# One-hot factors of a gate table in pair-major order, and products of two token pairs in one operation

## The chip, the cores and the metric

The kernel runs on one core of a Trainium2 chip. The metric is the device time of one execution in microseconds (us); the median of several runs is compared. The engines of a core work from queues of their own and meet at semaphores: PE (TensorE) multiplies matrices, with its weight loads shown as PEld; DVE (VectorE), ACT (ScalarE) and POOL (GpSimd) work element by element; SP issues most DMAs.

## The reference, cut to what matters

One decoder layer on 528 positions (16 learned ones and 512 tokens) of width 1024: a mixer (a chunked state-space scan beside a gated short convolution), then a retrieval feed-forward, then a norm. The change lies in the feed-forward, `peer_ffn`:

```python
s = einsum('thsd,hskd->thsk', q, sub_keys)          # 8 heads, 2 halves, 128 keys
v_half, i_half = top_k(s, 16)
cand = v_half[:, :, 0, :, None] + v_half[:, :, 1, None, :]
best, pos = top_k(cand.reshape(T, 8, 256), 16)
i1 = take_along_axis(i_half[:, :, 0], pos // 16);  i2 = take_along_axis(i_half[:, :, 1], pos % 16)
experts = i1 * 128 + i2                             # 8 x 16 = 128 of 16384 experts per token
gates = softmax(best)
act = gelu(einsum('td,tkd->tk', x, expert_u[experts])) * gates
out = einsum('tk,tkd->td', act, expert_v[experts])
```

## The kernel before, in words

The mixer takes the first 450 us or so. The feed-forward treats the tokens in four tiles of 128. Tile 0 is done sparsely: its experts' rows are fetched by indirect DMA (`fetch`, `dot`, `weigh`, `addv`). Tiles 1 to 3, 384 tokens, are done densely: for each of 128 blocks b of 128 experts, `z_unit` computes gelu(u_b x) for all 384 tokens (24 matmuls at L699, one activation at L775), multiplies it by the gates of that block (`h_unit`), and multiplies by v_b (`vmm`, L1009). Where an expert isn't among a token's 128, its gate is zero.

So the dense part needs a table of gates, experts by tokens, in DRAM (`gd`). It is made tile by tile, in two steps:

- `select(tt)` finds the lists of a tile (the first index i1, the second i2, the gate, for 128 slots a token), transposes them so that slots lie on partitions, and builds one-hot factors in f16. i1 is cut into its high part xa (0 to 7) and low part xb (0 to 15). `ob` is the one-hot of xb (16 x 128 tokens), `oa` that of xa (8 x 128), and `oag` is oa times the gate, once with the gate's high f16 part and once with its low part (16 x 128). `x2` holds i2.
- `gates(tt, c)` takes 16 tokens at a time (a chunk, TC = 16; 8 chunks a tile, 24 in all), in four groups of four. For every two groups one DVE operation makes `o2`, the one-hot of i2 over 128 keys (L886). For every group DVE makes `o1`, per slot the products oag x ob of four tokens, 512 numbers a pair of tokens. Then for each token two matmuls (L898, one for each part of the gate) contract over the slots, and give that token's 128 x 128 gates in PSUM; ACT copies them into `stg` (L901), and SP writes a chunk's stg into `gd` (L902).

Tokens are handled in pairs that lie next to each other in memory, 4 bytes in f16. `o1` has NO1 = 4 buffers of four tokens, the PSUM tile `pR` six, `stg` two. The factor tiles are stored with tokens innermost, [slot, x, token]; the step tables they are compared with are `iota16` (16 x 128) and `iota128` (128 x 2), both made by POOL.

While the tables are made, dense blocks go on as far as there is room: 36 blocks (`EARLYZ`) are computed early. Five come before the first chunk, 26 are spread over the 24 chunks, and five follow the last chunk (`z_early`, in the driver loop). Their weights are split into a high and a low part as they arrive (`Stream.prep_upto`: ACT at L88, then DVE or POOL at L90). The rest of `select` for the next tile is interleaved with the first chunks of a tile (L836 to L841 are its lookups by one-hot).

Within an engine, instructions run in the order in which the program was scheduled; the scheduler places them by its own estimate of when each can run. So a change in one operation can move its neighbours. PE's queue interleaves L898 with L699, DVE's the products with the splits and the selection.

Of the kernel before, what the change touches and what calls it, by code (L numbers as in the profile page):

```python
# [8 lines left out]
F16 = mybir.dt.float16  # L9
# [3 lines left out]
ALU = mybir.AluOpType  # L13
# [4 lines left out]
P = 128  # L18
# [653 lines left out]
def peer(tc, top, nc, st, small, dram, h, n2s, rs2, g_ffn_row, ident, keys, uv, g_final, out, rstd_of):  # L672
    dma = nc.sync.dma_start
    act = nc.scalar.activation
    V = nc.vector
# [12 lines left out]
    rp = r1.enter_context(tc.tile_pool(name="rp", bufs=2))  # L688
    psR = r1.enter_context(tc.tile_pool(name="psR", bufs=6, space=PSUM, reuse_waits="tile"))

    def proj(kind, b, spans):
        ps = [psZ.tile([P, T], F32, name="pZ") for _ in spans]
        cnt = [0] * len(spans)
        for i in range(2):
            wp = st.next((kind, b), i)
            for s, (o0, o1) in enumerate(spans):
                for k in range(4):
                    for a_, b_ in PASSES:
                        mm(ps[s][:, :o1 - o0], wp[a_][:, k * P:(k + 1) * P], n2s[b_][:, 4 * i + k, o0:o1],  # L699
                           start=cnt[s] == 0, stop=cnt[s] == 23)  # L700
                        cnt[s] += 1
        return ps

    iota128 = rp.tile([P, P, 2], F16, name="iota128", bufs=1)
    nc.gpsimd.iota(iota128, pattern=[[1, P], [0, 2]], base=0, channel_multiplier=0,
                   allow_small_or_imprecise_dtypes=True)
    iota16 = rp.tile([P, 16, P], F16, name="iota16", bufs=1)
    nc.gpsimd.iota(iota16, pattern=[[1, 16], [0, P]], base=0, channel_multiplier=0,
                   allow_small_or_imprecise_dtypes=True)
# [14 lines left out]
    def top2(tt, j):  # L724
        best, pos, cand = bests[tt][:, j], poss[tt][:, j], cands.pop((tt, j))
        V.max(best[:, 0:8], cand)
        V.max_index(pos[:, 0:8], best[:, 0:8], cand)
        V.match_replace(cand, best[:, 0:8], cand, -3.0e38)
        V.max(best[:, 8:16], cand)
        V.max_index(pos[:, 8:16], best[:, 8:16], cand)  # L730
# [13 lines left out]
    for j in range(16):  # L744
        kt = qp.tile([P, P], F32, name="kt")
        dma(out=kt, in_=keys[j])
        p = qps.pop(j) if j in qps else proj("q", j, ((0, T),))[0]
        qT = qp.tile([P, T], F32, name="qT")
        act(qT, p, AF.Copy)
        p = psR.tile([P, 512], F32, name="pR")  # L750
# [16 lines left out]
    rp = r1.enter_context(tc.tile_pool(name="rp3", bufs=2))  # L767
# [23 lines left out]
    def ut_(nm, n=P):  # L791
        return rp.tile([P, n], U32, name=nm, bufs=1)

    def ft(nm, n=P):
        return rp.tile([P, n], F32, name=nm, bufs=1)
# [4 lines left out]
    def select(tt):  # L800
        x16, best, pos = x16s[tt], bests[tt], poss[tt]
        xT = rp.tile([P, 2, 16, 8], F16, name="xT", bufs=1)
        nc.gpsimd.tensor_copy(xT, x16.rearrange("p (h s) x -> p s x h", s=2))
        if tt in EARLY:
            top2(tt, 7)
        else:
            for j in range(8):
                cand2(tt, j, V)
                top2(tt, j)
                if j % 3 == 2:  # L810
                    yield
        lists = rp.tile([P, 3, P], F32, name="lists", bufs=1)

        def kh(ap):
            return ap.rearrange("p (k h) -> p h k", h=8)

        def hk(ap):
            return ap.rearrange("p (h k) -> p h k", k=16)

        pf = pos.rearrange("p h k -> p (h k)")  # L820
        pe, pa, pd, pb = ut_("pe"), ut_("pa"), ut_("pd"), ut_("pb")
        V.tensor_scalar(pe, pf, 2, None, ALU.logical_shift_right)
        V.tensor_scalar(pa, pf, 4, None, ALU.logical_shift_right)
        V.tensor_scalar(pd, pf, 12, None, ALU.bitwise_and)
        V.tensor_scalar(pb, pf, 15, None, ALU.bitwise_and)
        m, t_, u_ = ft("pm"), ft("pt"), ft("pu")
        ij = rp.tile([P, 2, P], F16, name="ij", bufs=1)
        V.tensor_scalar(m, pf, 64.0, None, ALU.is_ge)
        V.scalar_tensor_tensor(t_, pe, -12.0, pa, ALU.add, ALU.subtract)
        V.tensor_tensor(t_, t_, m, ALU.mult)  # L830
        V.tensor_tensor(kh(ij[:, 0]), hk(t_), hk(pa), ALU.add)
        V.tensor_tensor(u_, pd, m, ALU.mult)
        V.tensor_tensor(kh(ij[:, 1]), hk(pb), hk(u_), ALU.subtract)
        for s in range(2):
            oh = rp.tile([P, 16, P], F16, name="oh", bufs=1)
            V.tensor_tensor(oh, iota16, ij[:, s, None, :].broadcast_to([P, 16, P]), ALU.is_equal)  # L836
            ohv = oh.rearrange("p x (k h) -> p x k h", h=8)
            V.tensor_tensor(ohv, ohv, xT[:, s, :, None, :].broadcast_to([P, 16, 16, 8]), ALU.mult)
            for n in (8, 4, 2):
                V.tensor_tensor(oh[:, 0:n], oh[:, 0:n], oh[:, n:2 * n], ALU.add)  # L840
            V.tensor_tensor(lists[:, s], oh[:, 0], oh[:, 1], ALU.add)  # L841
            yield
        ge = rp.tile([P, 8, 16], F32, name="ge", bufs=1)
        V.tensor_tensor(ge, best, best[:, :, 0:1].broadcast_to([P, 8, 16]), ALU.subtract)
        act(ge, ge, AF.Exp)
        gs = small.tile([P, 8], F32, name="gs")
        V.tensor_reduce(gs, ge, AX.X, ALU.add)
        V.reciprocal(gs, gs)
        V.tensor_tensor(kh(lists[:, 2]), ge, gs[:, :, None].broadcast_to([P, 8, 16]), ALU.mult)
        if tt < NGT:  # L850
            xid = xids[tt]
            V.scalar_tensor_tensor(xid[0], lists[:, 0], float(P), lists[:, 1], ALU.mult, ALU.add)
            nc.gpsimd.tensor_copy(xid[1], lists[:, 2])
            return
        p = psR.tile([P, 512], F32, name="pR")
        for i in range(3):
            nc.tensor.transpose(p[:, i * P:(i + 1) * P], lists[:, i], ident)
        gh, gl = (rp.tile([P, P], F16, name="gh") for _ in range(2))
        act(gh, p[:, 2 * P:3 * P], AF.Copy, scale=GS)
        V.scalar_tensor_tensor(gl, p[:, 2 * P:3 * P], GS, gh, ALU.mult, ALU.subtract)  # L860
        x2 = rp.tile([P, P], F16, name="x2")
        xa, xb = (rp.tile([P, P], F16, name="xa") for _ in range(2))
        act(x2, p[:, P:2 * P], AF.Copy)
        iu, ia = ut_("iu"), ut_("ia")
        V.tensor_copy(iu, p[:, 0:P])
        V.tensor_scalar(ia, iu, 4, None, ALU.logical_shift_right)
        V.tensor_scalar(iu, iu, 15, None, ALU.bitwise_and)
        V.tensor_copy(xa, ia)
        V.tensor_copy(xb, iu)
        ob = rp.tile([P, 16, P], F16, name="ob")  # L870
        V.tensor_tensor(ob, iota16, xb[:, None, :].broadcast_to([P, 16, P]), ALU.is_equal)
        oa = rp.tile([P, 16, P], F16, name="oh", bufs=1)[:, 0:8]
        V.tensor_tensor(oa, iota16[:, 0:8], xa[:, None, :].broadcast_to([P, 8, P]), ALU.is_equal)
        oag = rp.tile([P, 16, P], F16, name="oag")
        for w, g_ in enumerate((gh, gl)):
            V.tensor_tensor(oag[:, 8 * w:8 * w + 8], oa, g_[:, None, :].broadcast_to([P, 8, P]), ALU.mult)
        lts[tt] = (x2, ob, oag)

    def gates(tt, c):
        x2, ob, oag = lts[tt]  # L880
        stg = rp.tile([P, NB, TC], F32, name="stg")
        for q in range(TC // 4):
            t0 = c * TC + 4 * q
            if q % 2 == 0:
                o2 = rp.tile([P, 4, P, 2], F16, name="o2", bufs=2)
                V.tensor_tensor(o2, iota128[:, None].broadcast_to([P, 4, P, 2]),  # L886
                                x2[:, t0:t0 + 8].rearrange("p (q t) -> p q t", t=2)[:, :, None, :]
                                .broadcast_to([P, 4, P, 2]), ALU.is_equal)
            o1 = rp.tile([P, 2, 16, 16, 2], F16, name="o1", bufs=NO1)
            for j in range(2):  # L890
                t1 = t0 + 2 * j
                V.tensor_tensor(o1[:, j], oag[:, :, None, t1:t1 + 2].broadcast_to([P, 16, 16, 2]),  # L892
                                ob[:, None, :, t1:t1 + 2].broadcast_to([P, 16, 16, 2]), ALU.mult)
            p = psR.tile([P, 512], F32, name="pR")
            for i in range(4):
                j = 2 * (q % 2) + i // 2
                for w in range(2):
                    mm(p[:, i * P:(i + 1) * P], o2[:, j, :, i % 2],  # L898
                       o1[:, i // 2, 8 * w:8 * w + 8].rearrange("p a b t -> p (a b) t")[:, :, i % 2],
                       start=w == 0, stop=w == 1)  # L900
            act(stg[:, :, 4 * q:4 * q + 4], p.rearrange("p (t i) -> p i t", t=4), AF.Copy, scale=1.0 / GS)  # L901
        dma(out=gd[(tt - NGT) * (P // TC) + c], in_=stg)  # L902
# [192 lines left out]
```

## Time and profile before

| | |
|---|---|
| median of 3 runs | 1767.74 us (1766.79 to 1767.86) |
| the profiled execution's own time | 1769.16 us |
| its span | 1767.5 us |
| PE busy, DVE busy over the span | 1699.3 us, 1373.0 us |
| product operations L892 | 192, busy 109.7 us |
| gate matmuls L898 | 768, busy 74.1 us |

The span is the time between the first and the last recorded instruction; the execution's time has some overhead around it. Busy time is the time in which an engine had at least one instruction running; instructions of one engine overlap at their ends, so that a mean duration times a count can be more than the busy time. PE's matmuls are pipelined, and a matmul that waits for its weights counts as busy.

### The profile page before, as it was taken

How to read it: one execution, taken by the hardware profiler on the slowest of the kernel's cores; microseconds unless marked ns; L12 is line 12 of the kernel's file. 1: busy time of each engine (PE TensorE's matmuls, PEld its weight loads, DVE VectorE, ACT ScalarE, POOL GpSimd, SP SyncE). 2: the span in 40 equal slices, each digit the busy share in tenths (PEclk: the TensorE clock that was granted, in tenths of full speed). 3: DMA queues.
4: the chain of work that ended last, by engine and by line, in shares of the span. 5: the costliest groups of instructions: out<-in, count | busy, mean ns of one | idle time of the engine just before them, and what ended most of it. 6: DMA issues, size and time to landing. Idle time of an engine off the chain costs nothing.

```text
span 1767.5 us, 27063 instructions
## 1 busy us (share of the span) xinstructions
PE 1699.3 (96%) x9549; PEld 1516.8 (86%) x9549; DVE 1373.0 (78%) x2914; ACT 783.0 (44%) x1546; POOL 602.1 (34%) x540
## 2 busy tenths in 40 slices
PE   7899999999999789889999999999999999999997
PEld 6899998977888777778999999999999999999886
DVE  6756468897599999997787777777878776776876
ACT  7444443355533444545444444443434444444343
POOL 3333235440345310224343333333233333333442
PEclk9999999999999899999999999999999999999999
DMA  4222221135422245557989888888888888898772
GB/s 149 72 72 63 81 84 61 60 120 190 159 96 83 82 146 204 199 196 271 335 319 328 310 299 322 311 292 328 307 306 318 315 319 297 315 324 319 266 250 96
DMA packets 132306, 382.92 MB, mean 217 GB/s; under 512 B 10425, under 2 KB 65337, under 8 KB 112713
## 3 DMA queue, kind: packets, MB, share of 16 engines
q1 hardware_dynamic: 113736, 246.96, 41.1%
q0 software_dynamic: 18432, 134.23, 19.7%
q8 instruction: 75, 1.23, 0.3%
q14 instruction: 63, 0.51, 0.1%
HBM read 351.13 MB, written 30.02 MB: 216 GB/s over the span
## 4 chain that ended last, share of the span: by engine, by line
PE 75%; DVE 20%; issue 2%; ACT 1%; DMA 1%; SPq 0%; POOL 0%; DVEq 0%; ACTq 0%; POOLq 0%
PE pV L1009 30%; PE pZ L699 24%; PE pA L293 8%; DVE o L892 5%; PE pA L433 4%; PE pA L590 4%; DVE w L90 1%; DVE o L886 1%; DVE x L761 1%; DVE w L390 1%; DVE x L758 1%; DVE ssb L759 1%; PE pS L522 1%; DVE v L760 1%; DVE v L757 1%
## 5 line engine op out<-in xcount | busy, mean ns | idle before, releaser
L699 PE MATMUL pZ<-n,w 128*128 128x384 f32 (+1 forms) x3408 | 670.8, 349 | 7.0 <-ACT zg L775 5.8
L699 PEld LDWEIGHTS pZ<-n,w 128*128 128x128 f32 x3408 | 610.2, 190 | 29.4 <-ACT zg L775 6.2
L90 POOL TENSOR_TENSOR w<-raw,w 128x512 fp32r<-128x512 f32 x210 | 301.5, 1440 | 752.0 <-ACT w L88 270.6
L1009 PE MATMUL pV<-w,hh 128*128 128x512 f32 x2304 | 540.7, 390 | 0.0
L90 DVE TENSOR_TENSOR w<-raw,w 128x512 fp32r<-128x512 f32 (+2 forms) x447 | 314.3, 706 | 277.8 <-PE pV L1009 173.5
L88 ACT ACTIVATE w<-raw 128x512 fp32r<-128x512 f32 (+1 forms) x657 | 404.0, 620 | 253.9 <-issue 93.6
L1009 PEld LDWEIGHTS pV<-w,hh 128*128 128x128 f32 x2304 | 431.6, 188 | 86.2
L293 PE MATMUL pA<-nT,w 128*128 128x272 f32 (+3 forms) x1488 | 207.4, 296 | 1.0 <-POOL w L90 0.5
L293 PEld LDWEIGHTS pA<-nT,w 128*128 128x128 f32 (+1 forms) x1488 | 192.1, 188 | 5.9 <-ACT nT L281 0.9
L948 DVE SCALAR_TENSOR_TENSOR h<-row,a,h 128x1024 f32<-128x1024 f32 x128 | 168.8, 1319 | 0.0
L938 DVE SCALAR_TENSOR_TENSOR row<-row,n2k 128x1024 f32<-128x1024 f32 x128 | 159.0, 1245 | 2.1 <-DMA row<-in_uv,xid 2.1
L932 POOL DMA_INDIRECT row<-in_uv,xid x128 | 133.1, 1039 | 24.7 <-issue 7.8
L984 ACT ACTIVATE hh<-hh 128x384 fp32r<-128x384 f32 x128 | 67.3, 525 | 144.8 <-PE pV L1009 89.5
L775 ACT ACTIVATE zg<-pZ 128x384 f32<-128x384 f32 x128 | 62.5, 488 | 139.6 <-PE pZ L699 134.7
L892 DVE TENSOR_TENSOR o<-oag,ob 128x512 f16<-128x512 f16 x192 | 109.7, 628 | 0.0
L898 PE MATMUL pR<-o,o 128*128 128x128 f16 x768 | 74.1, 222 | 20.5 <-DVE o L892 11.4
L898 PEld LDWEIGHTS <-o 128*128 128x128 f16 x768 | 49.2, 98 | 50.6 <-DVE o L892 29.9
L496 POOL TENSOR_TENSOR sr<-aS,ut 128x384 fp32r<-128x384 f32 x64 | 62.8, 999 | 84.7 <-PE pS L498 43.3
L982 DVE TENSOR_TENSOR hh<-zg,gt 128x384 f32<-128x384 f32 x128 | 86.6, 676 | 4.5 <-DMA gt<-gd 1.2
L985 DVE TENSOR_TENSOR hh<-hh 128x384 fp32r<-128x384 f32 x128 | 87.1, 680 | 2.6 <-ACT hh L984 2.4
L943 ACT ACTIVATE a<-z 128x1 f32<-128x1 f32 x128 | 25.9, 202 | 139.9 <-DVE row L938 139.9
L901 ACT ACTIVATE stg<-pR 128x512 f32<-128x512 f32 x96 | 57.0, 598 | 68.7 <-PE pR L898 60.7
(232 smaller groups left out, 1521.1 us busy)
## 6 DMA issues: line engine op xcount, KB each, us to landing
raw<-in_u_t SPq DMA_DIRECT2D x128, 512.0 KB, 4.7
raw<-in_uv SPq DMA_DIRECT2D x128, 512.0 KB, 5.2
gd<-stg SPq DMA_DIRECT2D x24, 1024.0 KB, 6.1
gt<-gd SPq DMA_DIRECT2D x16, 1536.0 KB, 13.3
raw<-in_w_out SPq DMA_DIRECT2D x32, 512.0 KB, 3.5
raw<-in_w_xbc SPq DMA_DIRECT2D x20, 512.0 KB, 3.5
raw<-in_w_q SPq DMA_DIRECT2D x16, 512.0 KB, 3.4
raw<-in_w_z SPq DMA_DIRECT2D x16, 384.0 KB, 3.0
```

The lines of the kernel that those rows point to most:

```text
L88: nc.scalar.activation(hi, r, AF.Copy)
L90: ins = (nc.gpsimd if on_pool else nc.vector).tensor_tensor(lo, r, hi.bitcast(F32), ALU.subtract)
L293: mm(p[:m, :o1 - o0], wp[a][:, c0:c0 + m], nTs[b][:, k, o0:o1], start=i == 0, stop=i == 3 * KD - 1)
L699: mm(ps[s][:, :o1 - o0], wp[a_][:, k * P:(k + 1) * P], n2s[b_][:, 4 * i + k, o0:o1], start=cnt[s] == 0, stop=cnt[s] == 23)
L892: V.tensor_tensor(o1[:, j], oag[:, :, None, t1:t1 + 2].broadcast_to([P, 16, 16, 2]), ob[:, None, :, t1:t1 + 2].broadcast_to([P, 16, 16, 2] ...
L898: mm(p[:, i * P:(i + 1) * P], o2[:, j, :, i % 2], o1[:, i // 2, 8 * w:8 * w + 8].rearrange("p a b t -> p (a b) t")[:, :, i % 2], start=w = ...
L932: nc.gpsimd.indirect_dma_start(out=row.rearrange("p a d -> p (a d)"), out_offset=None, in_=uv, in_offset=bass.IndirectOffsetOnAxis(ap=xids ...
L938: V.scalar_tensor_tensor(row[:, 0], row[:, 0], 1.0, n2k[:, tt], ALU.mult, ALU.mult, accum_out=z)
L948: V.scalar_tensor_tensor(h[:, tt, :], row[:, 1], a, h[:, tt, :], ALU.mult, ALU.add)
L982: V.tensor_tensor(hf_.rearrange("p (c t) -> p c t", t=TC), zg[b].rearrange("p (c t) -> p c t", t=TC), gts[b // GR][:, :, b % GR, :], ALU.mult)
L985: V.tensor_tensor(hl, hf_, hh.bitcast(F32), ALU.subtract)
L1009: mm(acc[tt, nh], hp_[a][:, ts_], vp_[w], start=b == 0 and q == 0, stop=b == NB - 1 and q == 2)
```

## The change

`ob` and `oag` are stored pair-major, [slot, pair of tokens, x, 2], and `oa` in the same way inside the tile of `oh`. They are compared with a small new table `iota2` (16 x 2), broadcast over the 64 pairs, where before `iota16` was used (which `select` still needs for its lookups). The two products of a group, one for each pair, become one operation over both pairs. The shape and layout of `o1`, the matmuls and everything behind them stay as they are.

```diff
+    iota2 = rp.tile([P, 16, 2], F16, name="iota2", bufs=1)
+    nc.gpsimd.iota(iota2, pattern=[[1, 16], [0, 2]], base=0, channel_multiplier=0,
+                   allow_small_or_imprecise_dtypes=True)
...
-        ob = rp.tile([P, 16, P], F16, name="ob")
-        V.tensor_tensor(ob, iota16, xb[:, None, :].broadcast_to([P, 16, P]), ALU.is_equal)
-        oa = rp.tile([P, 16, P], F16, name="oh", bufs=1)[:, 0:8]
-        V.tensor_tensor(oa, iota16[:, 0:8], xa[:, None, :].broadcast_to([P, 8, P]), ALU.is_equal)
-        oag = rp.tile([P, 16, P], F16, name="oag")
+        def pairs(ap, n):
+            return ap.rearrange("p (q t) -> p q t", t=2)[:, :, None, :].broadcast_to([P, P // 2, n, 2])
+
+        def steps(n):
+            return iota2[:, None, 0:n, :].broadcast_to([P, P // 2, n, 2])
+
+        ob = rp.tile([P, P // 2, 16, 2], F16, name="ob")
+        V.tensor_tensor(ob, steps(16), pairs(xb, 16), ALU.is_equal)
+        oa = rp.tile([P, 16, P], F16, name="oh", bufs=1)[:, 0:8].rearrange("p x (q t) -> p (x q t)", t=2)
+        oa = oa.rearrange("p (q x t) -> p q x t", x=8, t=2)
+        V.tensor_tensor(oa, steps(8), pairs(xa, 8), ALU.is_equal)
+        oag = rp.tile([P, P // 2, 16, 2], F16, name="oag")
         for w, g_ in enumerate((gh, gl)):
-            V.tensor_tensor(oag[:, 8 * w:8 * w + 8], oa, g_[:, None, :].broadcast_to([P, 8, P]), ALU.mult)
+            V.tensor_tensor(oag[:, :, 8 * w:8 * w + 8, :], oa, pairs(g_, 8), ALU.mult)
...
-            for j in range(2):
-                t1 = t0 + 2 * j
-                V.tensor_tensor(o1[:, j], oag[:, :, None, t1:t1 + 2].broadcast_to([P, 16, 16, 2]),
-                                ob[:, None, :, t1:t1 + 2].broadcast_to([P, 16, 16, 2]), ALU.mult)
+            V.tensor_tensor(o1, oag[:, t0 // 2:t0 // 2 + 2, :, None, :].broadcast_to([P, 2, 16, 16, 2]),
+                            ob[:, t0 // 2:t0 // 2 + 2, None, :, :].broadcast_to([P, 2, 16, 16, 2]), ALU.mult)
```

Before the changed lines the program's order is the same on every engine, and so it is in the main loop but for its first blocks. In between it moves. DVE's queue in the first tile's second chunk, beside the selection of the next tile, stood so before (tiles by name, a number where several buffers share it; L840 and L841 belong to the selection):

```order
L840 TENSOR_TENSOR oh<-oh 128x1024
L886 TENSOR_TENSOR o_6880<-iota_5087,x_6511 128x1024
L840 TENSOR_TENSOR oh<-oh 128x512
L892 TENSOR_TENSOR o_6882<-oag,ob 128x512
L840 TENSOR_TENSOR oh<-oh 128x256
L892 TENSOR_TENSOR o_6882<-oag,ob 128x512
L841 TENSOR_TENSOR lists<-oh 128x128
L892 TENSOR_TENSOR o_6895<-oag,ob 128x512 x2
L886 TENSOR_TENSOR o_6908<-iota_5087,x_6511 128x1024
```

and stands so now, nine lines further down in the code (L897 is L886, L901 is L892, L843 and L844 are L840 and L841):

```order
L843 TENSOR_TENSOR oh<-oh 128x1024
L897 TENSOR_TENSOR o_6878<-iota_5087,x_6513 128x1024
L843 TENSOR_TENSOR oh<-oh 128x512
L901 TENSOR_TENSOR o_6880<-oag,ob 128x1024
L843 TENSOR_TENSOR oh<-oh 128x256
L901 TENSOR_TENSOR o_6892<-oag,ob 128x1024
L844 TENSOR_TENSOR lists<-oh 128x128
L897 TENSOR_TENSOR o_6904<-iota_5087,x_6513 128x1024
```

A group's product is one entry where it was two, and the second group's product now comes ahead of L844. On PE the end of the first group of gate matmuls and the start of the second stood so before:

```order
L898 LDWEIGHTS o_6715
L898 MATMUL pR<-o_6717,o_6715 128x128
L699 MATMUL pZ<-n_4674,w 128x384
L898 LDWEIGHTS o_6715
L898 MATMUL pR<-o_6730,o_6715 128x128
```

and now, where the first three groups follow each other and L699 comes behind the third:

```order
L907 LDWEIGHTS o_6743
L907 MATMUL pR<-o_6745,o_6743 128x128
L699 MATMUL pZ<-n_4674,w 128x384
L907 LDWEIGHTS o_6743
L907 MATMUL pR<-o_6757,o_6743 128x128
```

Over the whole stage the 768 gate matmuls (L907, before L898) stand in 60 runs between the L699 matmuls, where they stood in 86.

## Prediction

> **What bounds the kernel now.** I read the page first for the engines' totals, then cut the span into stages, then looked at the stage that holds the edited lines: what its operations cost, and who waits there for whom. The page's first lines:
>
> ```profile
> span 1767.5 us, 27063 instructions
> PE 1699.3 (96%) x9549; PEld 1516.8 (86%) x9549; DVE 1373.0 (78%) x2914; ACT 783.0 (44%) x1546; POOL 602.1 (34%) x540
> ```
>
> PE looks like the bound of the whole, at 96%. That is an average over stages, so the next view gives busy time by stage (start:end, length, then each engine, the granted TensorE clock, the DMA share, GB/s):
>
> ```profile
> 480.00:612.00 132.00, 122.97 (x614) 104.49 (x613) 126.84 (x795) 48.38 (x82) 65.43 (x104) 0.95 0.26 88
> 612.00:818.00 206.00, 184.35 (x1385) 153.22 (x1384) 205.16 (x405) 103.77 (x186) 50.46 (x3) 0.98 0.53 189
> 818.00:845.00 27.00, 27.00 (x154) 27.00 (x153) 13.04 (x21) 12.15 (x23) 4.02 (x3) 1.00 0.90 289
> 845.00:1767.00 922.00, 912.64 (x4493) 818.94 (x4492) 690.82 (x1108) 382.91 (x798) 320.34 (x253) 1.00 0.83 299
> ```
>
> The edited lines run from 612 to 818 us. There DVE is busy 205.16 of 206 us, and PE is idle 206 - 184.35 = 21.65 us. In the two stages behind it PE is busy for 27 of 27 and 912.64 of 922 us. So the gate stage alone is set by DVE; what it loses in length, the later stages should keep. In the waits of this stage (us in total, times, longest) PE's queue stands behind the one product operation, and DVE stands behind almost nothing:
>
> ```profile
> PEld L898 <- DVE o L892: 29.9, 75, 2.9
> PE pR L898 <- DVE o L892: 11.4, 14, 2.6
> DVE w L90 <- ACT w L88: 0.4, 1, 0.4
> ```
>
> **The products (the term that matters).** The stage issues L892 192 times and L886 48 times:
>
> ```profile
> L892 DVE TENSOR_TENSOR o<-oag,ob 128x512 f16<-128x512 f16 x192 | 109.7, 628 | 0.0
> L886 DVE TENSOR_TENSOR o<-iota,x 128x1024 f16<-128x1024 f16 x48 | 33.6, 700 | 0.0
> ...
> ```
>
> The mean durations overlap: the next operation starts before the one in front has ended. The price on a full engine is the distance from start to start, read from the timeline (start, length, engine, line):
>
> ```profile
> 617.55 4.34 DVE L892 TENSOR_TENSOR o<-oag,ob 128x512 f16<-128x512 f16 x8
> 621.82 1.21 DVE L836 TENSOR_TENSOR oh<-iota,ij 128x2048 f16<-128x2048 f16 x1
> ...
> 696.04 1.21 DVE L838 TENSOR_TENSOR oh<-oh,xT 128x2048 f16<-128x2048 f16 x1
> 697.18 0.67 DVE L886 TENSOR_TENSOR o<-iota,x 128x1024 f16<-128x1024 f16 x1
> 697.78 0.67 DVE L840 TENSOR_TENSOR oh<-oh 128x1024 f16<-128x1024 f16 x1
> 698.38 0.61 DVE L892 TENSOR_TENSOR o<-oag,ob 128x512 f16<-128x512 f16 x1
> 698.92 0.41 DVE L840 TENSOR_TENSOR oh<-oh 128x512 f16<-128x512 f16 x1
> 699.26 0.61 DVE L892 TENSOR_TENSOR o<-oag,ob 128x512 f16<-128x512 f16 x1
> ```
>
> Eight products take 621.82 - 617.55 = 4.27 us, 0.535 each. L840 on plain contiguous rows takes 698.38 - 697.78 = 0.60 us for 1024 elements and 699.26 - 698.92 = 0.34 for 512. That makes 0.508 ns per element and 0.08 us fixed. A product of 512 elements thus costs 0.195 us more than its size asks for. What sets it apart is how it reads: each pair of elements (4 bytes) of ob lies 256 bytes from the next, and oag's pair is a lone one too, repeated 16 times. L886 also repeats a lone pair, 128 times, but beside a contiguous table, and still takes 0.60 for 1024. After the change ob is read as runs of 32 contiguous elements, and oag's pair repeats 16 times beside it: L886 with its two inputs exchanged. So I price the new product, 1024 elements, at 0.60 us. Its bounds are 0.60 and 1.12 (1024 elements singly at 2 x 0.508 ns, plus 0.08). I take the low end, since L886 is the nearest row.
>
> 96 new products replace 192: 96 x (2 x 0.535 - 0.60) = 96 x 0.47 = 45.1 us of DVE work. DVE then needs about 206 - 45 = 161 us for the stage.
>
> [...]
>
> **How much of that reaches the end.** PE is next, and its busy time hides waiting. Its price per matmul where it does not wait:
>
> ```profile
> 612.00:818.00 206.00, 134.12 (x611) 107.21 (x610) 0.98 0.53 189
> 612.00:818.00 206.00, 74.05 (x768) 49.25 (x768) 0.98 0.53 189
> ...
> 700.66 0.40 PE L898 MATMUL pR<-o,o 128*128 128x128 f16 x4
> 700.87 0.42 PE L699 MATMUL pZ<-n,w 128*128 128x384 f32 x1
> ...
> 816.48 13.85 PE L699 MATMUL pZ<-n,w 128*128 128x384 f32 x77
> ```
>
> The first two rows are the stage once for L699 alone and once for L898 alone. Unhindered, 77 matmuls of L699 take 13.85 us, 0.18 each, and four of L898 0.21 us, 0.052 each. PE therefore needs 611 x 0.18 + 768 x 0.052 = 150 us. Both engines would fit the stage into about 161 us, if they never waited for each other. They will: o1 still has four buffers of four tokens, so DVE can be one group of 16 tokens ahead at most, and where the selection of the next tile stands between products (L836 to L841), PE's queue still stops. The lower bound on the gain is PE's visible idle time, 21.65 us; the upper one DVE's 45.1. I take 30, because PE's weight loads now wait 29.9 us for exactly this product; those waits have their cause removed, and they lie between the bounds. The stage would become 176 us.
>
> **The rest, costed at or near nothing.** The three builds of ob, oa and oag keep their element counts. Their old rows run pairwise, and the new ones read short contiguous runs and a repeated pair as L886 does, so zero; bounds: a tenth better, or the singly-priced case of the last rival. The rows in question, and the new table's neighbour on POOL:
>
> ```profile
> L876 DVE TENSOR_TENSOR oag<-oh,gh 128x1024 f16<-128x1024 f16 x6 | 3.9, 687 | 0.0
> L871 DVE TENSOR_TENSOR ob<-iota,xa 128x2048 f16<-128x2048 f16 x3 | 3.7, 1220 | 0.0
> L873 DVE TENSOR_TENSOR oh<-iota,xa 128x1024 f16<-128x1024 f16 x3 | 2.1, 687 | 0.0
> ...
> 476.82 1.53 POOL L705 IOTA iota<- 128x256 f16 x1 [7.60 <-PE pS L245]
> 478.31 1.93 POOL L708 IOTA iota<- 128x2048 f16 x1
> 480.21 6.00 POOL L90 TENSOR_TENSOR w<-raw,w 128x512 fp32r<-128x512 f32 x4
> ...
> 484.39 6.79 PE L699 MATMUL pZ<-n,w 128*128 128x512 f32 x28
> ```
>
> The added iota of 32 elements is placed on POOL between those two, and costs at most L705's 1.53 us. Behind it in POOL's queue wait four L90 halves. PE first needs one of them at 484.39; it ends at 480.21 + 1.5 = 481.7, so 2.7 us of cover. Without that cover it would cost 1.5 us.
>
> The new order also moves things. On PE the 768 gate matmuls now stand in 60 runs between the L699 matmuls instead of 86, always in eights, since a group's eight wait for one operation: the first four get their product 0.60 - 0.535 = 0.07 us later, the last four 0.47 earlier. That is inside the 161 to 184 us. On SP some writes of stg change place with loads of raw; the DMA engines are busy 0.53 of the stage, and would be 0.53 x 206 / 176 = 0.62, so I cost it at zero, with the later stage's 0.90 as the sign of how much there is left. No wait is added on any engine. Late next: in the stretches with selection PE still waits for DVE, in the others DVE for o1's buffers.
>
> **The sum.** Span 1767.5 - 30 = 1737.5. The profiled execution took 1769.16, 1.66 more than its span and 1.42 above the median of the runs, 1767.74. On the median's scale the forecast is 1767.7 - 30 = 1738 us.
>
> **Rivals.**
> 1. PE is the bound as its row shows it, and only its visible idle time goes: 12 to 24 us gained, 21.65 by the row, 1746 us. For it: PE busy 184.35 of 206. Against it: 1385 matmuls cost 150 us where nothing waits.
> 2. All of DVE's saving lands, 45.1 us: 1723 us. For it: 161 us is still above PE's 150. Against it: only four buffers lie between the engines.
> 3. The change doesn't do what it says: a lone pair still costs a step of its own when the other input is contiguous. A step then costs (0.535 - 0.08) / 256 = 1.78 ns, the product 512 x 1.78 + 80 ns = 0.99 us, and 96 x 0.08 = 7.7 us are gained: 1760 us. L886 speaks against it. [...]
> 4. Slower: patterns with a repeated dimension in both inputs fall to one element at a time. The product costs 1.12 against 1.07 us, 96 x 0.05 = 4.8; the builds at 0.508 ns more per element add 3 x 1.04 + 3 x 0.52 + 6 x 0.52 = 7.8; DVE sets the stage, so 1768 + 12.6 = 1780 us. It decides from 1.07 us per product on. For it: L892 itself, with repeats on both sides, costs 0.535, little under the 0.60 of 512 elements singly. Against it: it is under.
> 5. No change: DVE's freed time turns into waits for o1 and PE goes on as it did, 1768 us.
>
> **How the numbers follow.** Forecast (24 to 40 us gained) 0.50; rival 1 0.23; rival 2 0.10; rival 3 0.09; rival 4 0.04; rival 5 0.04. The likeliest gives 1738 us, its own range 1728 to 1744. Range: 1723 takes in nearly all of the full saving; above, 1756 takes in rival 1 down to 12 us gained and leaves rivals 3 to 5 out, 0.17. 0.2% (3.5 us) is about what a measurement of this kernel can tell from no change: faster by more 0.50 + 0.23 + 0.10 + 0.09 = 0.92, within 0.04, slower 0.04.
>
> **What would show it.** The product's row should have 96 of 1024 elements, start to start 0.60 us, mean near 700 ns like L886; about 1 us is rival 3, over 1.07 rival 4. DVE in the gate stage should be below full for the first time, and its waits name PE. The stage, from the first product to the last gate matmul, should be near 176 us; 184 with PE full is rival 1, 161 rival 2. The stages before and after should keep their lengths within 2 us; a longer stretch behind the stage, with the DMA share above 0.90, would mean that the gain was given back to loads, and would make the forecast wrong even with a cheap product.

## Result, and the profile after

The changed kernel takes 1726.9 us (median of 4 runs, 1725.46 to 1727.93) against 1767.76 (1766.79 to 1767.86): 40.9 us less, ratio 0.9771 with a 95% interval of 0.9759 to 0.9783. The forecast was 1738, the range 1723 to 1756.

The page's first lines, then the stages of the changed kernel, cut where the matching ones of before were cut (start:end, length, then busy time of each engine, clock, DMA share, GB/s):

```profile
span 1725.0 us, 26970 instructions
PE 1674.7 (97%) x9549; PEld 1510.8 (88%) x9549; DVE 1324.5 (77%) x2818; ACT 782.8 (45%) x1546; POOL 558.5 (32%) x541
```

```profile
480.00:610.50 130.50, 121.58 (x601) 102.66 (x601) 126.36 (x796) 47.08 (x80) 64.08 (x103) 0.95 0.28 89
610.50:774.00 163.50, 158.14 (x1375) 146.21 (x1374) 160.94 (x309) 100.15 (x185) 12.07 (x3) 0.99 0.65 235
774.00:801.00 27.00, 27.00 (x154) 27.00 (x154) 12.08 (x19) 12.44 (x24) 3.44 (x3) 1.00 1.02 318
801.00:1725.00 924.00, 914.22 (x4503) 820.44 (x4501) 686.74 (x1111) 385.88 (x800) 317.35 (x254) 1.00 0.83 298
```

The gate stage went from 206 to 163.5 us, 42.5 less, as much as the whole span lost (1767.5 to 1725.0). The stretch ahead of it kept its length within 2 us (130.5 against 132), and so did the two behind it (27 against 27, 924 against 922). In the stage DVE is still busy nearly all the time, 160.94 of 163.5 us; PE now is too, 158.14, for about the same number of matmuls. The row of the gate matmuls alone (PE, PEld, clock, DMA share, GB/s), which answers to the one of L898 before:

```profile
610.50:774.00 163.50, 56.20 (x768) 44.75 (x768) 0.99 0.65 235
```

The products, in the groups and in the timeline:

```profile
L901 DVE TENSOR_TENSOR o<-oag,ob 128x1024 f16<-128x1024 f16 x96 | 63.4, 685 | 0.0
```

```profile
615.91 2.49 DVE L901 TENSOR_TENSOR o<-oag,ob 128x1024 f16<-128x1024 f16 x4
618.32 1.22 DVE L839 TENSOR_TENSOR oh<-iota,ij 128x2048 f16<-128x2048 f16 x1
```

Four of them take 618.32 - 615.91 = 2.41 us, 0.60 each. The waits in the stage (us in total, times, longest), the lines that answer to those shown of before:

```profile
PEld L907 <- DVE o L901: 8.8, 26, 2.6
PE pR L907 <- DVE o L901: 4.1, 4, 2.3
DVE w L90 <- ACT w L88: 0.5, 1, 0.5
```

PE's waits for the product fell from 29.9 and 11.4 us to 8.8 and 4.1. DVE still waits for almost nobody: the row shown and 0.4 us of issue are all of its waits, and none of them is for PE.

### The profile page after: what moved, and what is told of

The parts are those of the page before. It is cut to its first block, busy times and chain, and to the rows that moved or that the text cites. A ratio compares the mean times of both kernels' runs of the same rounds, so it can differ in the third digit from the quotient of the medians.

```text
span 1725.0 us, 26970 instructions
## 1 busy us (share of the span) xinstructions
PE 1674.7 (97%) x9549; PEld 1510.8 (88%) x9549; DVE 1324.5 (77%) x2818; ACT 782.8 (45%) x1546; POOL 558.5 (32%) x541
## 4 chain that ended last, share of the span: by engine, by line
PE 83%; DVE 14%; issue 1%; ACT 1%; DMA 0%; SPq 0%; DVEq 0%; ACTq 0%
PE pV L1018 30%; PE pZ L699 29%; PE pA L293 9%; PE pA L590 4%; PE pA L433 4%; PE pR L907 2%; PE pS L522 1%; DVE x L764 1%; DVE w L390 1%; DVE ssb L762 1%; DVE x L761 1%; DVE v L763 1%; DVE v L760 1%; DVE w L388 1%; PE pS L498 1%
## 5 line engine op out<-in xcount | busy, mean ns | idle before, releaser
L699 PE MATMUL pZ<-n,w 128*128 128x384 f32 (+1 forms) x3408 | 661.6, 348 | 6.9 <-ACT zg L778 5.7
L699 PEld LDWEIGHTS pZ<-n,w 128*128 128x128 f32 x3408 | 608.1, 189 | 29.3 <-ACT zg L778 6.0
L90 POOL TENSOR_TENSOR w<-raw,w 128x512 fp32r<-128x512 f32 x210 | 298.7, 1426 | 780.6 <-ACT w L88 252.4
L90 DVE TENSOR_TENSOR w<-raw,w 128x512 fp32r<-128x512 f32 (+2 forms) x447 | 311.0, 698 | 288.4 <-PE pV L1018 187.6
L433 PE MATMUL pA<-w,nT 128*128 128x384 f32 x384 | 73.1, 348 | 0.0
L433 PEld LDWEIGHTS pA<-w,nT 128*128 128x128 f32 x384 | 69.1, 193 | 2.3 <-issue 1.6
L901 DVE TENSOR_TENSOR o<-oag,ob 128x1024 f16<-128x1024 f16 x96 | 63.4, 685 | 0.0
```

What stands on the lines that cost most here:

```text
L90: ins = (nc.gpsimd if on_pool else nc.vector).tensor_tensor(lo, r, hi.bitcast(F32), ALU.subtract)
L433: mm(pz[tt][:, :GW], nTs[b][:, k, t0:t0 + P], wz[a], start=k == 0 and i == 0, stop=k == KD - 1 and i == 2)
```

## Experiments

Times are medians; "before" in the same sessions was 1767.3 to 1768.3 us. A kernel's gate stage is given from the start of its first o2 operation to that of its last gate matmul, which is 204.2 us before and 162.9 in the changed kernel.

**1. Two products a group on the new layouts.** It tells the layout from the merging.

```diff
-            V.tensor_tensor(o1, oag[:, t0 // 2:t0 // 2 + 2, :, None, :]...,
-                            ob[:, t0 // 2:t0 // 2 + 2, None, :, :]..., ALU.mult)
+            for j in range(2):
+                u = t0 // 2 + j
+                V.tensor_tensor(o1[:, j], oag[:, u, :, None, :]..., ob[:, u, None, :, :]..., ALU.mult)
```

> The new layouts, but a group's products in two operations of 512 elements again. Reading theory (the price was ob's lone pairs): each operation starts 0.34 us after the one in front, 0.68 a group against 0.60, so DVE does 96 x 0.08 = 7.7 us more and the time is 1727 + 7 = 1734 us. Rival (the single operation, with the order that comes with it, is what gained): an operation stays at 0.535 us and the time goes back to 1760 or more.

1731.55 us (1729.96 to 1733.42). The timeline at the first products:

```profile
615.62 2.76 DVE L903 TENSOR_TENSOR o<-oag,ob 128x512 f16<-128x512 f16 x8
618.31 1.21 DVE L839 TENSOR_TENSOR oh<-iota,ij 128x2048 f16<-128x2048 f16 x1
```

2.69 us for eight, 0.336 each, where the old layout took 0.535 for the same 512 elements. So the layout alone brings 36 of the 41 us, and the merging the last 4.6.

**2 and 3. One factor at a time.** In 2 `ob` is pair-major and `oag` as before, in 3 the other way round; both with two products a group. The builds of the factors, which change with their layout, are left out of this diff.

```diff
 (2)
+                V.tensor_tensor(o1[:, j], oag[:, :, None, t1:t1 + 2]..., ob[:, t1 // 2, None, :, :]..., ALU.mult)
 (3)
+                V.tensor_tensor(o1[:, j], oag[:, t1 // 2, :, None, :]..., ob[:, None, :, t1:t1 + 2]..., ALU.mult)
```

> Only ob is stored pair-major; oag keeps tokens innermost, its lone pairs 256 bytes apart and each repeated 16 times; two operations of 512 a group. Reading theory (a repeated pair is not charged, ob's were): 0.34 us an operation, 1734 us, the same as with both layouts and two operations. Rival (oag's pairs are charged too, by their distance): 0.535 us, 1768 us; if half the price each, 0.44 us and 1751.

> Only oag is stored pair-major; ob keeps tokens innermost, lone pairs 256 bytes apart; two operations of 512 a group. Reading theory: 0.535 us an operation as before the change, 1768 us. Rival (oag's layout is what counts): 0.34 us and 1734.

1732.12 us (1730.98 to 1732.86) and 1766.06 (1761.46 to 1768.77). The products of 2 first, then of 3 (durations of one in ns: least, median, most):

```profile
L902 DVE TENSOR_TENSOR o<-oag,ob x192: 368/415/662, 615.4 to 777.5; 128x512 f16<-128x512 f16 x192
```

```profile
L903 DVE TENSOR_TENSOR o<-oag,ob x192: 551/603/742, 617.0 to 812.4; 128x512 f16<-128x512 f16 x192
```

The reading of ob was nearly the whole price. oag's lone pairs, 256 bytes apart but each repeated 16 times, cost little: with them 1732.1, without 1731.6; in 3 a product shortens from 624 to 603 ns, and the ratio to before is 0.9989 (0.9979 to 0.9999). The order of the work is no rival here: in the traces of before, 1, 2 and 3 the operations of PE, DVE and ACT follow each other in the same order, with the same tiles and shapes. POOL has one small iota more in 1, 2 and 3.

**4. Half of the o2 operations**, from the changed kernel. It takes more work off DVE, and leaves half of the one-hots of i2 out.

```diff
-            if q % 2 == 0:
+            if q == 0:
                 o2 = rp.tile([P, 4, P, 2], F16, name="o2", bufs=2)
```

> The changed kernel, but o2 made once in 16 tokens instead of twice, the second eight tokens using the first eight's: it leaves half of the one-hots of i2 out. DVE does 24 x 0.60 = 14.4 us less. If DVE alone still sets the stage: 1727 - 14 = 1713 us. If DVE and PE are both nearly full (DVE 161 of 163.5 us busy, PE 158): PE takes over, a gain of 3 to 8, 1719 to 1724, and DVE waits for o1's buffers. If PE sets it already: 1727.

1720.27 us (1718.8 to 1721.75): 14.4 us less on DVE bring 6.6. Its gate stage, and the wait that is new on DVE:

```profile
612.00:769.00 157.00, 155.17 (x1379) 147.59 (x1378) 147.57 (x286) 99.28 (x186) 11.49 (x3) 1.00 0.69 251
```

```profile
DVE w L90 <- PE pZ L699: 7.5, 8, 1.4
```

PE is busy 155.17 of 157 us, DVE only 147.57, and DVE's weight splits into `w` wait for L699, which reads `w`. Here PE has become the bound, at about 155 us. The expectation had DVE waiting for o1's buffers; it waits before its writes to `w`.

**5. Half of the gate matmuls**, from the changed kernel: PE's work instead of DVE's.

```diff
-                for w in range(2):
+                for w in range(1):
                     mm(p[:, i * P:(i + 1) * P], o2[:, j, :, i % 2], o1[...],
-                       start=w == 0, stop=w == 1)
+                       start=w == 0, stop=w == 0)
```

> The changed kernel without the second of the two gate matmuls of a token (the gate's low f16 part is left out of the table). PE's need in the gate stage falls by 384 x 0.058 = 22 us, to about 136; DVE's stays at 161. If DVE sets the stage of 163.5 us: 1724 to 1727 us. If PE sets it: 1705. If both are so close that each waits for the other at times: a gain of 3 to 8, 1719 to 1724.

1727.44 us (1724.18 to 1728.94), the changed kernel's time within the spread. An estimated 22 us less of PE's work (384 x 0.057, from the 32 gate matmuls that take 773.56 - 771.74 = 1.82 us in the changed kernel) brought nothing, which speaks for DVE as what sets the stage of the changed kernel. The stage (window 612 to 781 us) and its waits:

```profile
612.00:781.00 169.00, 152.85 (x1021) 133.98 (x1020) 161.34 (x309) 101.36 (x185) 12.69 (x3) 0.94 0.63 227
```

```profile
PEld L907 <- DVE o L901: 18.1, 29, 3.1
PE pR L907 <- DVE o L901: 12.8, 12, 2.9
DVE w L90 <- ACT w L88: 5.7, 9, 1.7
```

PE waits more for the product than in the changed kernel (8.8 and 4.1 us there). The stage itself was longer, 167.9 us, and the part behind it 4.8 shorter: with fewer gate matmuls the scheduler put more of the L699 matmuls ahead of the last of them (631 between 612 and 781 us, where the changed kernel has 601 in its stage). So a stage's length alone can mislead where the order moves; the time decides. The test is not a clean one: the granted clock in this stage was 0.94 (0.99 in the changed kernel), and DVE, busy 161.34 of 169 us, waits 5.7 us for ACT's part of the splits (0.5 there). What less PE work would bring at an equal clock is not shown.

**6. Two buffers for o1** instead of four (NO1 = 2).

> The changed kernel with two buffers for o1 instead of four, so that DVE can be eight tokens ahead of PE and not sixteen. If DVE is behind PE nearly everywhere, so that a buffer is free before DVE wants it (DVE waits 0 to 1 us for PE in the changed kernel): 1727 to 1731 us. If the buffers were what held the gain below 45 us: a loss of 10 us or more, 1737 to 1750.

1729.03 us (1728.25 to 1729.6), 2.1 more. DVE's groups of that stage, with the idle time before them:

```profile
L901 DVE TENSOR_TENSOR o<-oag,ob 128x1024 f16<-128x1024 f16 x96 | 63.3, 685 | 1.1 <-PE pR L907 1.1
L90 DVE TENSOR_TENSOR w<-raw,w 128x512 fp32r<-128x512 f32 x52 | 35.8, 689 | 2.4 <-PE pZ L699 1.4 <-ACT w L88 0.8 <-issue 0.2
```

Even with half of the buffers the products wait 1.1 us for one. With four they wait 0.0, so four were no limit at all.

**7. Each product issued twice**, from the changed kernel.

```diff
+            for _ in range(2):
                 V.tensor_tensor(o1, oag[...], ob[...], ALU.mult)
```

> The changed kernel with each product issued twice: 96 x 0.60 = 57.6 us more on DVE, whose need goes to 219 us, PE's stays at 150 to 158. If each us of DVE reaches the end while DVE's need is well above PE's: 1727 + 55 to 58 = 1782 to 1785 us. If PE and DVE share the cost as in the small steps around the changed kernel (5 of 7.7 us and 7 of 14.4): 0.5 to 0.6 of it, 1756 to 1762.

1775.12 us (1774.31 to 1775.44), 48.2 more for 57.6 us of DVE. Its stage is 218.2 us, 55.3 more, with DVE full again:

```profile
611.00:829.00 218.00, 183.44 (x1408) 165.48 (x1407) 217.20 (x403) 102.43 (x185) 52.26 (x3) 0.89 0.50 180
```

So the stage takes what DVE needs, nearly us for us; 7 of the 55 come back behind it, where fewer L699 matmuls are left (634 lie in the stage). The first theory, whose 55 to 58 us fit the stage, left that out; sharing the cost at 0.5 to 0.6 is ruled out. The granted clock was lower here too, 0.89, but PE is idle for 35 of the 218 us while DVE is full.

**8. Half of the weight splits on POOL** for the early blocks from the sixth on, from the changed kernel.

```diff
-            add(("z", b), u_t[b], pool=(n < ZPOOL, n < ZPOOL))
+            add(("z", b), u_t[b], pool=(n < ZPOOL, True))
```

> The changed kernel, with the second half of each early block's weight split (L90) on POOL instead of DVE for the blocks from the sixth on. In the gate stage DVE does 26 x 0.62 = 16 us less. If POOL does a half in its usual 1.4 us: as with half of o2, 1718 to 1722 us. If POOL is held up by a busy DVE as the cast xT was (5.5 us in this stage, 0.6 before it): 13 us a half against 6.3 us a block, PE waits for it, and the time goes up by 50 us or more.

1750.95 us (1746.81 to 1752.12), 24 more. That is slower, as the second theory had it, but not by its price: a split on POOL took 2.9 us on average in this stage and not 13. The stage's groups, and two pieces of its timeline:

```profile
L90 POOL TENSOR_TENSOR w<-raw,w 128x512 fp32r<-128x512 f32 x25 | 72.0, 2882 | 106.5 <-PE pZ L699 30.6 <-ACT w L88 22.2 <-DVE o L901 19.7
L901 DVE TENSOR_TENSOR o<-oag,ob 128x1024 f16<-128x1024 f16 x96 | 67.2, 724 | 0.0
```

```profile
680.71 1.29 POOL L90 TENSOR_TENSOR w<-raw,w 128x512 fp32r<-128x512 f32 x1 [2.83 <-PE pZ L699]
680.75 2.40 DVE L901 TENSOR_TENSOR o<-oag,ob 128x1024 f16<-128x1024 f16 x2
687.00 17.98 POOL L90 TENSOR_TENSOR w<-raw,w 128x512 fp32r<-128x512 f32 x1 [5.00 <-PE pZ L699]
```

```profile
703.97 1.56 DVE L897 TENSOR_TENSOR o<-iota,x 128x1024 f16<-128x1024 f16 x1
705.56 1.66 DVE L901 TENSOR_TENSOR o<-oag,ob 128x1024 f16<-128x1024 f16 x1
```

The same split takes POOL 1.29 us once and 17.98 another time, and DVE is busy throughout both. Beside the short one it is DVE that is held up: two products take 2.40 us, nearly what four take in the changed kernel (2.49), and the pair in the second piece takes more than twice its 0.68 us beside a split of about 1.7 us (two splits take 19.68 us from 687.00 on, the first of them 17.98). During the long one DVE's operations keep their usual lengths until its last microsecond (an L897 or L901 that stands alone 0.68 us from 687.25 to 701.97). So now the one engine is late and now the other; what decides which is not shown. Of the 25 splits in the stage, 72.0 us together, one took 17.98 us and two that follow each other from 653.96 us on took 14.88; the other 22 come to (72.0 - 17.98 - 14.88) / 22 = 1.8 us each. How much of the 24 us comes from the late splits, from the slower DVE, from the changed order and from the clock, 0.94 in this stage, stays open.

**9. Lone pairs 8 bytes apart.** `ob` and `oag` are woven into one tile, so that a pair of ob is followed by one of oag; two products a group.

```diff
-        ob = rp.tile([P, P // 2, 16, 2], F16, name="ob")
-        oag = rp.tile([P, P // 2, 16, 2], F16, name="oag")
+        both = rp.tile([P, P // 2, 16, 2, 2], F16, name="both")
+        ob, oag = both[:, :, :, 0, :], both[:, :, :, 1, :]
```

> The kernel with two products a group, but ob and oag woven into one tile, so that ob's pairs are lone ones again, now 8 bytes apart instead of 256 (before) or adjacent. [...] If a lone pair costs wherever the next one lies: 0.53 us a product, 1766 us and up to 5 more.

1731.85 us (1731.47 to 1733.04), as with adjacent pairs (1731.55) and 34 us below the 1766 of a lone pair that costs wherever the next one lies:

```profile
L903 DVE TENSOR_TENSOR o<-both x192: 368/418/667, 616.5 to 778.5; 128x512 f16<-128x512 f16 x192
```

```profile
616.49 2.77 DVE L903 TENSOR_TENSOR o<-both 128x512 f16<-128x512 f16 x8
619.17 1.22 DVE L839 TENSOR_TENSOR oh<-iota,ij 128x2048 f16<-128x2048 f16 x1
```

Eight of them take 619.17 - 616.49 = 2.68 us, 0.335 each.

In these runs a lone pair is not what costs; its distance is. A product on pairs 8 bytes apart takes as long as on adjacent ones (median 418 against 415 ns), on pairs 256 bytes apart 603 to 624 ns. Building the woven tile cost nothing more (1.22 us for ob's part, as before), so the up to 5 us allowed for it stayed out. Where between 8 and 256 bytes the price sets in wasn't tried.

**10 to 12. Products of eight tokens in one operation**, o1 in two buffers of eight, with the changed kernel beside it in a second session.

```diff
+            if q % 2 == 0:
+                o1 = rp.tile([P, 4, 16, 16, 2], F16, name="o1", bufs=NO1 // 2)
+                V.tensor_tensor(o1, oag[:, t0 // 2:t0 // 2 + 4, :, None, :].broadcast_to([P, 4, 16, 16, 2]),
+                                ob[:, t0 // 2:t0 // 2 + 4, None, :, :].broadcast_to([P, 4, 16, 16, 2]), ALU.mult)
...
-                       o1[:, i // 2, 8 * w:8 * w + 8]...
+                       o1[:, j, 8 * w:8 * w + 8]...
```

> The changed kernel with the products of eight tokens (four pairs) in one operation of 2048 elements, and o1 in two buffers of eight tokens. Such an operation takes 1.14 us from start to start against 2 x 0.60, so DVE does 48 x 0.06 = 2.9 us less: at the 0.5 to 0.6 that small steps around the changed kernel gave, 1725 us. If PE is hurt by getting tokens by eights with two buffers: 1728 to 1732.

> The changed kernel, run beside the next one on the same chip: 1727 us as before, within 2.

> Products of eight tokens in one operation, beside the changed kernel: if the 2 us that lay between them in separate rounds are real, 1725 us and 2 below its neighbour; if not, the two differ by less than 1 us.

1724.78 us (1723.8 to 1725.57), then 1724.89 (1724.66 to 1725.73) beside 1727.82 (1726.79 to 1728.19) for the changed kernel. The price of an operation, from the first of the two sessions:

```profile
615.24 2.35 DVE L902 TENSOR_TENSOR o<-oag,ob 128x2048 f16<-128x2048 f16 x2
617.51 1.22 DVE L839 TENSOR_TENSOR oh<-iota,ij 128x2048 f16<-128x2048 f16 x1
```

Two of them take 617.51 - 615.24 = 2.27 us, 1.14 each. The times of the two kernels don't overlap: 2.9 us less, as much as DVE saves by 48 x 0.06 = 2.9, where the expectation had reckoned with 0.5 to 0.6 of it. This version beats both kernels, at 0.9754 (0.974 to 0.9767) of before.

## Why the prediction was right in the direction and short in the size

- **The bound was named rightly.** The gate stage was set by DVE, and the stages behind it kept the gain. DVE sets it still: in 7 the stage takes what DVE needs, and 5 agrees as far as its other differences let it.
- **The price of a product was right:** 0.60 us forecast, 0.60 measured, and DVE's need 161 forecast, 160.94 busy. The reading of the trace behind it held too: ob's scattered pairs were the cost (2 against 3), and L886 was the right neighbour for a repeated pair. The rival that a lone pair still costs beside a contiguous input (0.99 us a product, 1760 us) and the slower one (1.12 us) fall with the product's row, the first also with 2. The slower one's price for elements read singly, 2 x 0.508 ns, is what the f32 split L90 shows before: 512 elements take 617.55 - 616.95 = 0.60 us from start to start, as 1024 of f16 do at L840. No change and PE as the bound (a stage of 184 us) fall with the result.
- **The step that failed is how much of it reaches the end.** "They will", that is, wait for each other, since four buffers allow DVE to be only 16 tokens ahead; so 30 us were taken out of 45.1 and the stage put at 176 us. It was 163.5, and 41 us reached the end. DVE never waited for a buffer, 0.0 us before the products: when a product started, all four buffers were in use at 9 of the 96, and at 33 no earlier product was left unread. Two buffers cost 2.1 us (6). Nor did PE's remaining stops hold the stage up, since DVE stayed full. The full-saving rival, 1723 us with a chance of 0.10, was the mechanism that came nearest. So the range held for a reason that the forecast itself did not favour: 1726.9 lies below the likeliest case's own 1728 to 1744, and inside the whole range because that was stretched to 1723 for this rival.
- **PE's 29.9 us of waiting was the wrong yardstick.** It is what PE's queue showed as waiting, and matmuls that waited counted as busy besides: the gate matmuls' busy time fell from 74.05 to 56.2 us with the same 768 of them. The rate of undisturbed stretches (150 us) was the better guide to PE's need; in experiment 4, where PE is the bound, it was busy for 155.
- **Rightly costed at nothing:** the iota of 32 elements took 0.29 us on POOL in its place, within the 2.7 us of cover. The three builds kept their prices (1216, 682 and 683 ns on average for ob, oa and oag, against 1220, 687 and 687). The gate stage starts 1.7 us earlier; POOL's first iota, which the same code leads up to in every run, starts anywhere between 474.5 and 477.4 us. The DMA share was 0.65 in the stage (0.62 forecast) and 1.02 in the 27 us behind it, which grew no longer.
- **Of the signs named, two failed with that step:** DVE was to be below full and to wait for PE, but it stayed at 98% and its waits don't name PE; that sign belongs to experiment 4, with 14 us less on DVE. And the stage was to be near 176 us; 163.5 is next to the 161 that was named as the sign of the full saving.

## What to carry to other kernels

When the longest wait is for an engine that is full from end to end of a stage, count what it does from start to start, and expect most of a cut in its work to reach the end as long as it needs more than the next engine does undisturbed; here 41 of 45 us did, and of the next 14.4, which took DVE below PE, 6.6. Ask whether the full engine waits for a buffer at all before counting the buffers as a limit. For the next engine's need, take the rate of a stretch that waits for nothing, not the busy time. And price an element-wise operation against a neighbour of the same size and type: 0.195 us over it, at equal element count, was the sign that its reading and not its arithmetic took the time.

## What was not expected of the hardware

A product of 512 elements that reads pairs of f16 values 256 bytes apart takes DVE 0.535 us from start to start; with adjacent pairs it takes 0.336, and with pairs 8 bytes apart 0.335. Where each pair is repeated 16 times, 256 bytes between the pairs are nearly free (median 415 ns a product with them in 2 as without in 1). And a split on POOL took from 1.28 to 17.98 us beside DVE's work, while DVE's operations took up to 1.75 us instead of 0.68 beside some of the short ones (the product at 707.82 us, beside a split of 1.33 from 707.69).
